# A LoRA-augmented linear layer on one core: rounding and copying in larger pieces, with TensorE looping over groups of 16 rows

## The chip, the core and the metric

The kernel runs on one core of a Trainium2 chip. The core has five engines with queues of their own (TensorE or PE, VectorE or DVE, ScalarE or ACT, GpSimd or POOL, SyncE or SP), and 16 DMA engines move data between the main memory and its on-chip memory. The metric is the device time of one execution in microseconds; lower is better. Before the change the median of three runs is 164.73 us (164.71 to 164.86).

## The reference

`x` is 16 x 2048 x 256 in float32, flattened to 32768 rows of 256. `W` is 256 x 256, `lora_A` 256 x 16, `lora_B` 16 x 256, `lora_E` has 16 numbers and `scale` is 1.

```
y = x_flat @ W
lora_out = ((x_flat @ lora_A) * lora_E) @ lora_B
y = y + scale * lora_out
```

All of it is one product with the 256 x 256 matrix `W + scale * (A * E) @ B`. About 33.5 MB are read and as many written.

## The kernel before

**Rows and chunks.** The 32768 rows are seen as 256 blocks of 128, here called rows for short: one row of the plan is one row of `x` on each of the 128 partitions, 128 KB in all. `PLAN` (line 10) cuts the 256 into seven chunks. A chunk of b rows is one load and one store, in which each partition's part is b KB in one piece. The chunks lie in a ring `xy` of 192 rows in on-chip memory (line 54); the results `y` overwrite the rows of `x` they come from. The first five chunks fill the ring. Chunks 5 and 6 reuse the places of chunks 0, 1 and 2.

**SP's queue** (lines 125 to 136) sets the order of the transfers: `W`, the loads of chunks 0 to 4, the stores 0, 1 and 2, the load of chunk 5 (once stores 0 and 1 have landed), the load of chunk 6 (once store 2 has landed), then the stores 3 to 6. A store is issued when `s_rdy` says that the chunk's last result is in the ring. `lora_A`, `lora_B` and `lora_E` come through ACT's queue (lines 189 to 191).

**The weights.** PE transposes `A` (line 219), DVE multiplies by `E` and `scale` (line 155), PE multiplies by `B` (line 223), DVE adds `W` and rounds to bf16 as `weff` (line 161).

**Steps.** The rows are worked on in steps of Q = 4 rows. DVE rounds eight rows at a time to bf16 into one of two buffers `xb` (line 173), one pair of steps ahead. PE transposes a step's four rows (line 202); bf16 pairs are moved as one float32. DVE copies the transposes from PSUM to `xt` (line 184). PE multiplies: eight matmuls a step, two of them for each row (line 210). ACT copies the step's `y` from PSUM into the ring (line 194), and after a chunk's last step it drains and signals `s_rdy` (line 196). PE's order is written out by hand (`turn`, line 226): the transposes of step k + 1 stand before the products of step k, in a loop over four steps at a time. `ps_xt` and `ps_y` have two halves each; `s_y` counts the copied ones.

**The pause.** Before it rounds the first rows of chunk `PAUSE` = 4, DVE waits until store 2 has landed (line 170). Since it rounds one pair of steps ahead, the last two steps of chunk 3 wait with it. At the start DVE runs 60 empty instructions (line 149).

Of the kernel before, what the change touches and what calls it, by code (L numbers as in the profile page):

```python
# [6 lines left out]

PLAN = [16, 32, 48, 48, 48, 48, 16]  # L10

RING = 192

LEAD = 5
AFTER = {2: [5, 6]}

PAUSE = 4

Q = 4


@with_exitstack
def kernel(
# [11 lines left out]
    P = 128  # L35
    FP32 = mybir.dt.float32
    BF16 = mybir.dt.bfloat16
# [3 lines left out]
    N, K = x_flat.shape  # L41
    M = out_flat.shape[1]
    R = lora_B.shape[0]
    KC = K // P
    CHUNKS = len(PLAN)
    assert K == M == KC * P and sum(PLAN) * P == N and all(b % (2 * Q) == 0 for b in PLAN)

    def sbuf(name, shape, dt):
        return ctx.enter_context(nc.sbuf_tensor(name, shape, dt))

    def psum(name, shape, dt):
        return ctx.enter_context(nc.psum_tensor(name, shape, dt))

    xy = sbuf("xy", [P, RING, K], FP32)

    late = sbuf("late", [P, Q * K], FP32)
    w_sb = late[:, :KC * M].rearrange("p (c m) -> p c m", c=KC)
    b_sb = late[:R, 2 * M:3 * M]
    b_bf = late[:R, 3 * M:3 * M + M // 2].bitcast(BF16)
    ate = late[:R, 3 * M + M // 2:4 * M].bitcast(BF16).rearrange("r (c p) -> r c p", c=KC)  # L60
    xb = [
        sbuf("xb0", [P, 2 * Q, K], BF16)[:],
        late.bitcast(BF16).rearrange("p (j k) -> p j k", k=K),
    ]

    xt = [sbuf(f"xt{s}", [P, Q, P, KC], BF16) for s in range(2)]
    a_sb = sbuf("a_sb", [P, KC, R], FP32)
    e_sb = sbuf("e_sb", [R, 1], FP32)
    weff = sbuf("weff", [P, KC, M], BF16)
    ident = sbuf("ident", [P, P], FP32)  # L70

    ps_xt = [psum(f"ps_xt{s}", [P, Q, P], FP32) for s in range(2)]
    ps_y = [psum(f"ps_y{s}", [P, Q, M], FP32) for s in range(2)]
    ps_at = psum("ps_at", [P, KC, P], FP32)
    ps_aeb = psum("ps_aeb", [P, KC, M], FP32)

    sem = tc.alloc_semaphore
    s_w, s_a, s_b, s_e = sem("s_w"), sem("s_a"), sem("s_b"), sem("s_e")
    s_in = [sem(f"s_in{i}") for i in range(CHUNKS)]
    starts = [sum(PLAN[:i]) for i in range(CHUNKS)]  # L80
    places = [r % RING for r in starts]
    assert sum(PLAN[:LEAD]) <= RING and all(r + b <= RING for r, b in zip(places, PLAN))

    owners = {
        i: [j for j in range(LEAD) if places[j] < places[i] + PLAN[i] and places[i] < places[j] + PLAN[j]]
        for i in range(LEAD, CHUNKS)
# [5 lines left out]
    s_lora = sem("s_lora")  # L92
    s_lpe = sem("s_lpe")
    s_xb = sem("s_xb")
    s_t = sem("s_t")
    s_xt = sem("s_xt")
    s_p = sem("s_p")
    s_y = sem("s_y")
    s_rdy = sem("s_rdy")

    def rows_of(flat, i):
        b, r0 = PLAN[i], starts[i] * P
        return flat[r0:r0 + b * P, :].rearrange("(p b) k -> p b k", b=b)
# [2 lines left out]
        return xy[:, places[i]:places[i] + PLAN[i], :]  # L106


    steps = [(i, r) for i, b in enumerate(PLAN) for r in range(0, b, Q)]

    def rows_of_step(k):
        i, r = steps[k]
        return xy[:, places[i] + r:places[i] + r + Q, :]

    n = len(steps)
    assert n % 4 == 0

    with tc.tile_critical(sync_engine=mybir.EngineType.SP, no_gpsimd_drain=True):  # L118
        sp, pe, dve, act, pool = nc.sync, nc.tensor, nc.vector, nc.scalar, nc.gpsimd


        def load(i):
            sp.dma_start(out=ring_of(i), in_=rows_of(x_flat, i)).then_inc(s_in[i], 16)

        sp.dma_start(out=w_sb, in_=W.rearrange("(p c) m -> p c m", c=KC)).then_inc(s_w, 16)
        for i in range(LEAD):
            load(i)
        for i in range(CHUNKS):
            sp.wait_ge(s_rdy, i + 1)
            sp.dma_start(out=rows_of(out_flat, i), in_=ring_of(i)).then_inc(s_out[min(i, again)], 16)  # L130
            for later in AFTER.get(i, []):
                for j in owners[later]:
                    sp.wait_ge(s_out[j], 16)
                load(later)
        for i in range(len(s_out) - 1):
            sp.wait_ge(s_out[i], 16)


        pool.memset(ident[:], 0.0).then_inc(s_id, 1)  # L139
        pool.wait_ge(s_id, 1)  # L140
        pool.affine_select(  # L141
            out=ident[:], in_=ident[:], compare_op=mybir.AluOpType.not_equal, fill=1.0,
            base=0, pattern=[[-1, P]], channel_multiplier=1,
        ).then_inc(s_id, 1)

        for _ in range(60):
            dve.nop()  # L150
        dve.wait_ge(s_b, 16)
        dve.tensor_copy(out=b_bf, in_=b_sb).then_inc(s_lora, 1)  # L152
        dve.wait_ge(s_e, 16)
        dve.wait_ge(s_lpe, 1)
        dve.tensor_scalar(  # L155
            out=ate, in0=ps_at[:R, :KC, :], scalar1=e_sb[:], scalar2=float(scale),
            op0=mybir.AluOpType.mult, op1=mybir.AluOpType.mult,
        ).then_inc(s_lora, 1)
        dve.wait_ge(s_w, 16)
        dve.wait_ge(s_lpe, 2)  # L160
        dve.tensor_add(out=weff[:], in0=w_sb, in1=ps_aeb[:]).then_inc(s_lora, 1)  # L161

        def round_steps(k):
            i, r = steps[k]
            if r == 0:
                dve.wait_ge(s_in[i], 16)
            if r == 0 and i == PAUSE:
                dve.wait_ge(s_out[again - 1], 16)  # L170
            if k == 2:
                dve.wait_ge(s_lora, 3)
            rounded = dve.tensor_copy(  # L173
                out=xb[k // 2 % 2], in_=xy[:, places[i] + r:places[i] + r + 2 * Q, :],
            )
            if k == 0:
                rounded.then_inc(s_xb, 1)

        round_steps(0)
        for k in range(n):  # L180
            if k % 2 == 0 and k + 2 < n:
                round_steps(k + 2)
            dve.wait_ge(s_t, k + 1)
            dve.tensor_copy(  # L184
                out=xt[k % 2][:].rearrange("w j p c -> w j (p c)"), in_=ps_xt[k % 2][:].bitcast(BF16),
            ).then_inc(s_xt, 1)


        act.dma_start(out=a_sb[:], in_=lora_A.rearrange("(p c) r -> p c r", c=KC)).then_inc(s_a, 16)
        act.dma_start(out=b_sb, in_=lora_B).then_inc(s_b, 16)  # L190
        act.dma_start(out=e_sb[:], in_=lora_E[:, None]).then_inc(s_e, 16)
        for k, (i, r) in enumerate(steps):
            act.wait_ge(s_p, k + 1)
            act.copy(out=rows_of_step(k), in_=ps_y[k % 2][:]).then_inc(s_y, 1)  # L194
            if r + Q == PLAN[i]:
                act.drain().then_inc(s_rdy, 1)

        def transposes(k):  # L200
            for j in range(Q):
                t = pe.transpose(  # L202
                    ps_xt[k % 2][:, j, :], xb[k // 2 % 2][:, k % 2 * Q + j, :].bitcast(FP32), ident[:],
                )
            t.then_inc(s_t, 1)

        def products(k):
            for j in range(Q):
                for c in range(KC):
                    m = pe.matmul(  # L210
                        ps_y[k % 2][:, j, :], xt[k % 2][:, j, :, c], weff[:, c, :],
                        start=(c == 0), stop=(c == KC - 1),
                    )
            m.then_inc(s_p, 1)

        pe.wait_ge(s_a, 16)
        pe.wait_ge(s_id, 2)
        for c in range(KC):
            t = pe.transpose(ps_at[:R, c, :], a_sb[:, c, :], ident[:])  # L219
        t.then_inc(s_lpe, 1)  # L220
        pe.wait_ge(s_lora, 2)
        for c in range(KC):
            m = pe.matmul(ps_aeb[:, c, :], ate[:, c, :], b_bf, start=True, stop=True)  # L223
        m.then_inc(s_lpe, 1)

        def turn(k):
            pe.wait_ge(s_xt, 1).then_inc(s_xt, -1)  # L227
            transposes(k + 1)
            pe.wait_ge(s_y, 1).then_inc(s_y, -1)
            products(k)  # L230

        pe.sem_inc(s_y, 2)
        pe.wait_ge(s_xb, 1)
        transposes(0)
        pe.wait_ge(s_lora, 3)

        with pe.Fori(0, n // 4):
            for k in range(4):
                turn(k)


    with tc.tile_critical(sync_engine=mybir.EngineType.SP, no_gpsimd_drain=True):
        nc.sync.wait_ge(s_out[again], 16 * (CHUNKS - again))

# [1 line left out]
_INS = ['x', 'W', 'lora_A', 'lora_B', 'lora_E', 'scale']  # L246
# [31 lines left out]
```

## Time and profile before

| What | us |
|---|---|
| median of the runs | 164.73 |
| the profiled execution | 166.16 |
| its span, which the profile's times refer to | 164.4 |
| PE busy | 104.0 |
| DVE busy | 79.6 |
| ACT busy | 66.2 |
| ACT's copy of `y`, 128x1024 f32, mean of 64 | 1.014 |
| DVE's copy of transposes, 128x1024 bf16, mean of 64 | 0.688 |
| DVE's rounding, 128x2048 to bf16, mean of 32 | 1.218 |
| DVE's wait for store 2 at the pause | 19.7 |

The profile is one execution, and its own time differs from the median of the runs. Its slices cut the span into 40 equal parts; a digit is the share of a slice in which an engine was busy, in tenths. PEclk is the clock granted to TensorE in tenths of full speed. An entry in the list of waits names who waited, for whom, how long in all, how often, and the longest. A DMA issue is listed with the time from its issue to its landing, which includes the time it stands behind others. In a table of windows each line gives start and end, then the busy time and number of instructions of PE, PEld, DVE, ACT and POOL, the granted clock, the DMA engines' share and GB/s.

### The profile page before, as it was taken

How to read it: one execution, taken by the hardware profiler on the slowest of the kernel's cores; microseconds unless marked ns; L12 is line 12 of the kernel's file. 1: busy time of each engine (PE TensorE's matmuls, PEld its weight loads, DVE VectorE, ACT ScalarE, POOL GpSimd, SP SyncE). 2: the span in 40 equal slices, each digit the busy share in tenths (PEclk: the TensorE clock that was granted, in tenths of full speed). 3: DMA queues.
4: the chain of work that ended last, by engine and by line, in shares of the span. 5: the costliest groups of instructions: out<-in, count | busy, mean ns of one | idle time of the engine just before them, and what ended most of it. 6: DMA issues, size and time to landing. Idle time of an engine off the chain costs nothing. (4 is left out here: it accounts for less than half of the span.)

```text
span 164.4 us, 1979 instructions
## 1 busy us (share of the span) xinstructions
PE 104.0 (63%) x776; PEld 80.6 (49%) x776; DVE 79.6 (48%) x99; ACT 66.2 (40%) x65; POOL 0.7 (0%) x6
## 2 busy tenths in 40 slices
PE   1039199899989998991000099999899899900000
PEld 0017178677767777770000087777777677700000
DVE  0181355768867886750000456788678767300000
ACT  3002224565666666563000026666656565620000
POOL 1000000000000000000000000000000000000000
PEclk9999957999999999999555559999999999975555
DMA  4999989998999898999899999899989999998970
GB/s 156 431 459 431 510 383 395 490 455 383 395 550 395 383 383 371 451 455 447 383 514 443 383 397 490 351 462 498 395 383 433 502 407 395 443 490 383 395 327 16
DMA packets 2370, 67.42 MB, mean 410 GB/s; under 512 B 432, under 2 KB 448, under 8 KB 576
## 3 DMA queue, kind: packets, MB, share of 16 engines
q1 hardware_dynamic: 2160, 67.37, 95.8%
q10 hardware_dynamic: 208, 0.03, 0.2%
q14 instruction: 2, 0.02, 0.0%
HBM read 33.85 MB, written 33.55 MB: 410 GB/s over the span
## 5 line engine op out<-in xcount | busy, mean ns | idle before, releaser
L194 ACT COPY xy<-ps_y 128x1024 f32<-128x1024 f32 x64 | 64.9, 1014 | 76.6 <-PE ps_y L210 76.6
L210 PE MATMUL ps_y<-weff,xt 128*128 128x256 bf16 x512 | 70.3, 283 | 0.0
L184 DVE COPY xt<-ps_xt 128x1024 bf16<-128x1024 bf16 x64 | 44.0, 688 | 30.6 <-PE ps_xt L202 30.5
L210 PEld LDWEIGHTS ps_y<-weff,xt 128*128 128x128 bf16 x512 | 52.1, 102 | 6.8
L202 PE MATMUL ps_xt<-ident,late 128*128 128x128 f32 x128 | 21.4, 293 | 26.7 <-PEq L227 26.7
L202 PEld LDWEIGHTS ps_xt<-ident,late 128*128 128x128 f32 x128 | 14.4, 148 | 34.5 <-issue 34.5
L173 DVE CAST xb<-xy 128x2048 bf16<-128x2048 f32 x16 | 19.5, 1218 | 24.3 <-DMA out_dram<-xy 19.7
L202 PE MATMUL ps_xt<-ident,xb 128*128 128x128 f32 x132 | 22.8, 300 | 5.9 <-PEq L227 3.9
L202 PEld LDWEIGHTS ps_xt<-ident,xb 128*128 128x128 f32 x132 | 15.8, 153 | 13.9 <-issue 11.1
L173 DVE CAST late<-xy 128x2048 bf16<-128x2048 f32 x16 | 19.5, 1217 | 0.0
L223 PE MATMUL ps_aeb<-late 16*128 16x256 bf16 x2 | 0.6, 404 | 3.8 <-DVE late L155 3.8
L219 PE MATMUL ps_at<-ident,a_sb 128*16 128x128 f32 x2 | 0.6, 402 | 3.5 <-DMA a_sb<-in_lora_A_dram 3.5
L152 DVE CAST late<-late 16x256 bf16<-16x256 f32 x1 | 0.3, 280 | 4.4 <-DMA late<-in_lora_B_dram 4.4
L223 PEld LDWEIGHTS ps_aeb<-late 16*128 16x128 bf16 x2 | 0.1, 106 | 4.3 <-DVE late L155 4.3
L194 ACT ACT_TABLE_LOAD x1 | 1.3, 1283 | 2.3 <-issue 2.3
L219 PEld LDWEIGHTS ps_at<-ident,a_sb 128*16 128x16 f32 x2 | 0.1, 90 | 3.5 <-DMA a_sb<-in_lora_A_dram 3.5
L155 DVE TENSOR_SCALAR late<-ps_at,e_sb 16x256 bf16<-16x256 f32 x1 | 0.5, 471 | 2.8 <-DMA e_sb<-in_lora_E_dram 2.8
L161 DVE TENSOR_TENSOR weff<-late,ps_aeb 128x512 bf16<-128x512 f32 x1 | 0.7, 687 | 0.8 <-PE ps_aeb L223 0.8
L141 POOL TENSOR_SCALAR_AFFINE_SELECT ident<-ident 128x128 f32<-128x128 f32 x1 | 0.3, 294 | 0.2 <-POOL ident L139 0.2
L139 POOL MEMSET ident<- 128x128 f32 x1 | 0.2, 205 | 0.5 <-SPq L118 0.5
L259 POOL MEMSET const-bfloat16-1.0<- 128x1 bf16 x1 | 0.1, 102 | 0.0
L259 POOL MEMSET const-uint8-127<- 128x1 uint8 x1 | 0.1, 102 | 0.0
(2 smaller groups left out, 0.2 us busy)
## 6 DMA issues: line engine op xcount, KB each, us to landing
xy<-in_x_dram SPq DMA_DIRECT2D x4, 6144.0 KB, 38.2
out_dram<-xy SPq DMA_DIRECT2D x4, 6144.0 KB, 26.1
xy<-in_x_dram SPq DMA_DIRECT2D x2, 2048.0 KB, 14.4
xy<-in_x_dram SPq DMA_DIRECT2D x1, 4096.0 KB, 17.1
out_dram<-xy SPq DMA_DIRECT2D x2, 2048.0 KB, 29.3
out_dram<-xy SPq DMA_DIRECT2D x1, 4096.0 KB, 37.8
late<-in_W_dram SPq DMA_DIRECT2D x1, 256.0 KB, 2.9
a_sb<-in_lora_A_dram ACTq DMA_DIRECT2D x1, 16.0 KB, 2.6
```

The source lines that it names most:

```text
L139: pool.memset(ident[:], 0.0).then_inc(s_id, 1)
L141: pool.affine_select(out=ident[:], in_=ident[:], compare_op=mybir.AluOpType.not_equal, fill=1.0, base=0, pattern=[[-1, P]], channel_multip ...
L152: dve.tensor_copy(out=b_bf, in_=b_sb).then_inc(s_lora, 1)
L155: dve.tensor_scalar(out=ate, in0=ps_at[:R, :KC, :], scalar1=e_sb[:], scalar2=float(scale), op0=mybir.AluOpType.mult, op1=mybir.AluOpType.mult,
L161: dve.tensor_add(out=weff[:], in0=w_sb, in1=ps_aeb[:]).then_inc(s_lora, 1)
L173: rounded = dve.tensor_copy(out=xb[k // 2 % 2], in_=xy[:, places[i] + r:places[i] + r + 2 * Q, :],)
L184: dve.tensor_copy(out=xt[k % 2][:].rearrange("w j p c -> w j (p c)"), in_=ps_xt[k % 2][:].bitcast(BF16),).then_inc(s_xt, 1)
L194: act.copy(out=rows_of_step(k), in_=ps_y[k % 2][:]).then_inc(s_y, 1)
L202: t = pe.transpose(ps_xt[k % 2][:, j, :], xb[k // 2 % 2][:, k % 2 * Q + j, :].bitcast(FP32), ident[:],)
L210: m = pe.matmul(ps_y[k % 2][:, j, :], xt[k % 2][:, j, :, c], weff[:, c, :], start=(c == 0), stop=(c == KC - 1),)
L219: t = pe.transpose(ps_at[:R, c, :], a_sb[:, c, :], ident[:])
L223: m = pe.matmul(ps_aeb[:, c, :], ate[:, c, :], b_bf, start=True, stop=True)
```

## The change

The plan becomes 16, 32, 48, 48, 32, 48, 32, and the ring 176 rows. DVE rounds G = 16 rows into the one buffer `xb`, and copies the transposes of S = 8 rows at a time. `ps_xt` then holds eight rows in each half; `ps_at` and `ps_aeb` share PSUM with `ps_y`. PE waits for `weff` before its first transpose and then loops over groups of 16 rows: all transposes of the group, then its products in four pieces of Q = 4 rows. ACT copies the first 58 pieces of `y`, and DVE the last `LATE` = 6, after all its other work. The last copy of a chunk signals `s_rdy` itself, without a drain; GpSimd passes that signal on to `s_y`, which is now one semaphore for each half of `ps_y`. The small inputs move to SP's queue: `lora_A` before chunk 0, `lora_B` and `lora_E` behind it. GpSimd rounds `lora_B`. The 60 empty instructions go.

```diff
-PLAN = [16, 32, 48, 48, 48, 48, 16]
-RING = 192
+PLAN = [16, 32, 48, 48, 32, 48, 32]
+RING = 176
...
-Q = 4
+G, S, Q = 16, 8, 4
+LATE = 6
...
-    late = sbuf("late", [P, Q * K], FP32)
...
-    xb = [
-        sbuf("xb0", [P, 2 * Q, K], BF16)[:],
-        late.bitcast(BF16).rearrange("p (j k) -> p j k", k=K),
-    ]
-    xt = [sbuf(f"xt{s}", [P, Q, P, KC], BF16) for s in range(2)]
+    xb = sbuf("xb", [P, G, K], BF16)
+    xt = [sbuf(f"xt{s}", [P, S, P, KC], BF16) for s in range(2)]
...
-    ps_xt = [psum(f"ps_xt{s}", [P, Q, P], FP32) for s in range(2)]
+    ps_xt = [psum(f"ps_xt{s}", [P, S, P], FP32) for s in range(2)]
     ps_y = [psum(f"ps_y{s}", [P, Q, M], FP32) for s in range(2)]
...
+    ps_at = ps_y[0][:R, 0, :].rearrange("r (c p) -> r c p", c=KC)
+    ps_aeb = ps_y[1][:, :KC, :]
...
-    s_y = sem("s_y")
+    s_y = [sem(f"s_y{h}") for h in range(2)]
...
+        sp.dma_start(out=a_sb[:], in_=lora_A.rearrange("(p c) r -> p c r", c=KC)).then_inc(s_a, 16)
+        load(0)
+        sp.dma_start(out=b_sb[:], in_=lora_B).then_inc(s_b, 16)
+        sp.dma_start(out=e_sb[:], in_=lora_E[:, None]).then_inc(s_e, 16)
+        for i in range(1, LEAD):
             load(i)
...
+        pool.wait_ge(s_b, 16)
+        pool.tensor_copy(out=b_bf[:], in_=b_sb[:]).then_inc(s_lora, 1)
...
+        copies = pieces(Q)
+        def y_of(q, engine, copy):
+            i, r = copies[q]
+            engine.wait_ge(s_p, q + 1)
+            done = copy(out=rows_at(i, r, Q), in_=ps_y[q % 2][:])
+            if r + Q == PLAN[i]:
+                done.then_inc(s_rdy, 1)
+            else:
+                done.then_inc(s_y[q % 2], 1)
+        for i in range(CHUNKS - 1):
+            pool.wait_ge(s_rdy, i + 1).then_inc(s_y[((starts[i] + PLAN[i]) // Q - 1) % 2], 1)
+        for q in range(len(copies) - LATE):
+            y_of(q, act, act.copy)
...
+        for g, (i, r) in enumerate(pieces(G)):
             if r == 0:
                 dve.wait_ge(s_in[i], 16)
             if r == 0 and i == PAUSE:
                 dve.wait_ge(s_out[again - 1], 16)
...
+            dve.tensor_copy(out=xb[:], in_=rows_at(i, r, G)).then_inc(s_xb, 1)
+            for k in range(g * G // S, (g + 1) * G // S):
+                dve.wait_ge(s_t, k + 1)
+                dve.tensor_copy(
+                    out=xt[k % 2][:].rearrange("w j p c -> w j (p c)"), in_=ps_xt[k % 2][:].bitcast(BF16),
+                ).then_inc(s_xt, 1)
+        for q in range(len(copies) - LATE, len(copies)):
+            y_of(q, dve, dve.tensor_copy)
...
-        act.dma_start(out=a_sb[:], in_=lora_A.rearrange("(p c) r -> p c r", c=KC)).then_inc(s_a, 16)
-        act.dma_start(out=b_sb, in_=lora_B).then_inc(s_b, 16)
-        act.dma_start(out=e_sb[:], in_=lora_E[:, None]).then_inc(s_e, 16)
...
-                act.drain().then_inc(s_rdy, 1)
...
         def products(k):
+            for h in range(S // Q):
+                pe.wait_ge(s_y[h], 1).then_inc(s_y[h], -1)
+                for j in range(Q):
+                    for c in range(KC):
+                        m = pe.matmul(
+                            ps_y[h][:, j, :], xt[k % 2][:, h * Q + j, :, c], weff[:, c, :],
+                            start=(c == 0), stop=(c == KC - 1),
+                        )
+                m.then_inc(s_p, 1)
...
-        def turn(k):
-            pe.wait_ge(s_xt, 1).then_inc(s_xt, -1)
-            transposes(k + 1)
-            pe.wait_ge(s_y, 1).then_inc(s_y, -1)
-            products(k)
...
         pe.wait_ge(s_lora, 3)
-        with pe.Fori(0, n // 4):
-            for k in range(4):
-                turn(k)
+        with pe.Fori(0, sum(PLAN) // G):
+            pe.wait_ge(s_xb, 1).then_inc(s_xb, -1)
+            for k in range(G // S):
+                transposes(k)
+            for k in range(G // S):
+                pe.wait_ge(s_xt, 1).then_inc(s_xt, -1)
+                products(k)
```

More of the change, by code (lines that the diff above doesn't have):

```diff
@@ L45 @@
     CHUNKS = len(PLAN)
-    assert K == M == KC * P and sum(PLAN) * P == N and all(b % (2 * Q) == 0 for b in PLAN)
+    assert K == M == KC * P and sum(PLAN) * P == N and all(b % G == 0 for b in PLAN)
     def sbuf(name, shape, dt):
@@ L54 @@
     xy = sbuf("xy", [P, RING, K], FP32)
-    late = sbuf("late", [P, Q * K], FP32)
[L57 to L60, printed above, removed]
-    xb = [
-        sbuf("xb0", [P, 2 * Q, K], BF16)[:],
-        late.bitcast(BF16).rearrange("p (j k) -> p j k", k=K),
-    ]
-    xt = [sbuf(f"xt{s}", [P, Q, P, KC], BF16) for s in range(2)]
+    xb = sbuf("xb", [P, G, K], BF16)
+    xt = [sbuf(f"xt{s}", [P, S, P, KC], BF16) for s in range(2)]
+    w_sb = sbuf("w_sb", [P, KC, M], FP32)
     a_sb = sbuf("a_sb", [P, KC, R], FP32)
+    b_sb = sbuf("b_sb", [R, M], FP32)
     e_sb = sbuf("e_sb", [R, 1], FP32)
+    b_bf = sbuf("b_bf", [R, M], BF16)
+    ate = sbuf("ate", [R, KC, P], BF16)
     weff = sbuf("weff", [P, KC, M], BF16)
     ident = sbuf("ident", [P, P], FP32)
-    ps_xt = [psum(f"ps_xt{s}", [P, Q, P], FP32) for s in range(2)]
+    ps_xt = [psum(f"ps_xt{s}", [P, S, P], FP32) for s in range(2)]
     ps_y = [psum(f"ps_y{s}", [P, Q, M], FP32) for s in range(2)]
-    ps_at = psum("ps_at", [P, KC, P], FP32)
-    ps_aeb = psum("ps_aeb", [P, KC, M], FP32)
+    ps_at = ps_y[0][:R, 0, :].rearrange("r (c p) -> r c p", c=KC)
+    ps_aeb = ps_y[1][:, :KC, :]
     sem = tc.alloc_semaphore
@@ L106, in ring_of, with pieces, rows_at @@
         return xy[:, places[i]:places[i] + PLAN[i], :]
[L109 to L116, printed above, removed]
+    def pieces(rows):
+        return [(i, r) for i, b in enumerate(PLAN) for r in range(0, b, rows)]
+    def rows_at(i, r, rows):
+        return xy[:, places[i] + r:places[i] + r + rows, :]
     with tc.tile_critical(sync_engine=mybir.EngineType.SP, no_gpsimd_drain=True):
@@ L123, in load @@
             sp.dma_start(out=ring_of(i), in_=rows_of(x_flat, i)).then_inc(s_in[i], 16)
-        sp.dma_start(out=w_sb, in_=W.rearrange("(p c) m -> p c m", c=KC)).then_inc(s_w, 16)
-        for i in range(LEAD):
+        sp.dma_start(out=w_sb[:], in_=W.rearrange("(p c) m -> p c m", c=KC)).then_inc(s_w, 16)
+        sp.dma_start(out=a_sb[:], in_=lora_A.rearrange("(p c) r -> p c r", c=KC)).then_inc(s_a, 16)
[3 more added lines that the diff above has]
+        for i in range(1, LEAD):
             load(i)
@@ L144 @@
         ).then_inc(s_id, 1)
[L149 to L152, printed above, removed]
+        pool.wait_ge(s_b, 16)
[13 more added lines that the diff above has]
+            y_of(q, act, act.copy)
         dve.wait_ge(s_e, 16)
@@ L155 @@
         dve.tensor_scalar(
-            out=ate, in0=ps_at[:R, :KC, :], scalar1=e_sb[:], scalar2=float(scale),
+            out=ate[:], in0=ps_at, scalar1=e_sb[:], scalar2=float(scale),
             op0=mybir.AluOpType.mult, op1=mybir.AluOpType.mult,
@@ L160 @@
         dve.wait_ge(s_lpe, 2)
-        dve.tensor_add(out=weff[:], in0=w_sb, in1=ps_aeb[:]).then_inc(s_lora, 1)
-        def round_steps(k):
-            i, r = steps[k]
+        dve.tensor_add(out=weff[:], in0=w_sb[:], in1=ps_aeb).then_inc(s_lora, 1)
+        for g, (i, r) in enumerate(pieces(G)):
             if r == 0:
@@ L170, in round_steps @@
                 dve.wait_ge(s_out[again - 1], 16)
[L171 to L186, printed above, removed]
@@ L189 @@
-        act.dma_start(out=a_sb[:], in_=lora_A.rearrange("(p c) r -> p c r", c=KC)).then_inc(s_a, 16)
-        act.dma_start(out=b_sb, in_=lora_B).then_inc(s_b, 16)
-        act.dma_start(out=e_sb[:], in_=lora_E[:, None]).then_inc(s_e, 16)
[L192 to L196, printed above, removed]
+            dve.tensor_copy(out=xb[:], in_=rows_at(i, r, G)).then_inc(s_xb, 1)
@@ L200, in transposes @@
+            for k in range(g * G // S, (g + 1) * G // S):
[5 more added lines that the diff above has]
+            y_of(q, dve, dve.tensor_copy)
         def transposes(k):
[L201 to L204, printed above, removed]
+            for j in range(S):
+                t = pe.transpose(ps_xt[k % 2][:, j, :], xb[:, k * S + j, :].bitcast(FP32), ident[:])
@@ L205, in transposes @@
             t.then_inc(s_t, 1)
         def products(k):
[L208 to L214, printed above, removed]
+            for h in range(S // Q):
[7 more added lines that the diff above has]
+                m.then_inc(s_p, 1)
@@ L216 @@
+        for h in range(2):
+            pe.sem_inc(s_y[h], 1)
         pe.wait_ge(s_a, 16)
@@ L218 @@
         for c in range(KC):
-            t = pe.transpose(ps_at[:R, c, :], a_sb[:, c, :], ident[:])
+            t = pe.transpose(ps_at[:, c, :], a_sb[:, c, :], ident[:])
         t.then_inc(s_lpe, 1)
@@ L222 @@
         for c in range(KC):
-            m = pe.matmul(ps_aeb[:, c, :], ate[:, c, :], b_bf, start=True, stop=True)
+            m = pe.matmul(ps_aeb[:, c, :], ate[:, c, :], b_bf[:], start=True, stop=True)
         m.then_inc(s_lpe, 1)
-        def turn(k):
-            pe.wait_ge(s_xt, 1).then_inc(s_xt, -1)
-            transposes(k + 1)
-            pe.wait_ge(s_y, 1).then_inc(s_y, -1)
-            products(k)
-        pe.sem_inc(s_y, 2)
-        pe.wait_ge(s_xb, 1)
-        transposes(0)
-        pe.wait_ge(s_lora, 3)
-        with pe.Fori(0, n // 4):
-            for k in range(4):
-                turn(k)
+        pe.wait_ge(s_lora, 3)
+        with pe.Fori(0, sum(PLAN) // G):
[5 more added lines that the diff above has]
+                products(k)
     with tc.tile_critical(sync_engine=mybir.EngineType.SP, no_gpsimd_drain=True):
```

## The prediction

> **What bounds the kernel now.** I read the slices first, because they show which resource is never idle, then the queue table, the waits of the queue that issues the transfers, the chain, and last narrow windows over the start and the end.
>
> ```profile
> DMA  4999989998999898999899999899989999998970
> DMA packets 2370, 67.42 MB, mean 410 GB/s; under 512 B 432, under 2 KB 448, under 8 KB 576
> ...
> q1 hardware_dynamic: 2160, 67.37, 95.8%
> ...
> PE ps_y L210 2%; PE ps_xt L202 2%; ACT xy L194 1%
> ```
>
> The DMA row is full from the second slice to the last but one; SP's queue holds the 16 DMA engines 95.8% of the span. The chain of work covers only 5% of the span: it ends with ScalarE's last copy at 145.03 us, and what follows is no engine's work but stores.
>
> ```profile
> SPq L130 <- ACTq L196: 105.9, 7, 23.4
> SPq L133 <- DMA out_dram<-xy: 18.0, 1, 18.0
> SPq L273 <- DMA out_dram<-xy: 16.8, 1, 16.8
> SPq L123 <- DMA out_dram<-xy: 14.2, 1, 14.2
> ```
>
> SP's sequencer does wait for copies (first line), but the transfers don't: a store that is issued lands 18 to 41 us later, since it stands behind others. The third line is the end: 16.8 us of waiting for stores already issued.
>
> ```profile
> 144.00:152.00 8.00, 0.00 (x0) 0.00 (x0) 0.00 (x0) 1.01 (x1) 0.00 (x0) 0.64 0.97 418
> ...
> 159.00:160.00 1.00, 0.00 (x0) 0.00 (x0) 0.00 (x0) 0.00 (x0) 0.00 (x0) 0.50 0.35 148
> 160.00:161.00 1.00, 0.00 (x0) 0.00 (x0) 0.00 (x0) 0.00 (x0) 0.00 (x0) 0.50 0.15 66
> 161.00:162.00 1.00, 0.00 (x0) 0.00 (x0) 0.00 (x0) 0.00 (x0) 0.00 (x0) 0.50 0.08 33
> ```
>
> Windows over the end (the last two columns are DMA share and GB/s): compute is over, and from 159 us only one or two of the 16 DMA engines still move bytes. So the bound is one queue, first in first out on each DMA engine, and inside it the engine that lags most.
>
> The packet records behind these windows give the budget. A 16, 32 or 48 KB packet takes 0.611, 1.213 or 1.815 us, and each engine carries eight of each load and store. Before: 16 x (2 x 0.611 + 1.213 + 4 x 1.815) = 155.1 us an engine. First x packets start at 3.2 to 3.8 us; 3.5 + 155.1 = 158.6. Most engines end at 159.3 to 159.8, the last at 162.6; it lands at 163.1 and the span ends at 164.4. What the last engine lost over 158.6 is 4.0 us: about 0.75 where the first stores follow the loads (its 48 KB packets at 60 us take 2.2 to 3.0), 1.2 on one packet at 93.6, 0.75 where loads turn to stores at 110 us, and 1.3 from store packets that take 1.90 for 1.82 as long as compute runs beside them, on one engine only.
>
> **The change, part by part.** PLAN 16 32 48 48 48 48 16 becomes 16 32 48 48 32 48 32. An engine's packets cost 16 x (0.611 + 3 x 1.213 + 3 x 1.815) = 155.1 us: **the same to a tenth**, with the same 14 big transfers and three turns between loads and stores. What can move is the edge.
>
> *Start.* lora_A's DMA goes ahead of chunk 0 on SP. Its issue took 0.39 us on ACT's queue; chunk 0 is issued at 1.38, its first packets follow W's (last W packet at 3.41). So the cost lies between 0 (W still fills the engines) and 0.45 us; I take 0.2. lora_B and E follow chunk 0: per engine a packet of 0.05 and one of 0.01 us, which ran before too, on the other queue, where the first chunk 0 packets beside them took up to 1.23 for 0.61. Between -0.2 and +0.2; I take 0. Their landing moves from 7.41 us (E) to about 10, behind chunk 0; the weights, by the rows between 7.43 and 9.36, are done 2 us later, at about 12, and TensorE now waits for them before its first transpose. That delays compute alone, which has the pause as cover (below).
>
> *DVE.* The rounding: 256 columns take 280 ns, 2048 take 1217, so 0.523 ns a column and 4096 take 2.29 us (for two of 1.22). The transposes' copy: 0.69 for 1024 columns, 1.22 for 2048 by the same slope (bounds 0.69 and 1.38). 4.73 us per 16 rows against 5.19. All of it lies beside transfers.
>
> *The new order on PE.* Four transposes take 0.63 and eight matmuls 0.87 at full clock (last chain), so 16 rows need 2.52 + 3.48 = 6.0, as before. But there is one xb, and products wait inside the group: copy of half one ends at 1.26 + 0.04 + 1.22 = 2.5, products start at 2.65 (0.12 from copy to the next PE work, as at 142.34 to 142.46). ps_y's two banks now go back by s_y[0] and s_y[1]: ScalarE's 1.01 per copy holds products 3 and 4 to about 4.7 and 5.7, the group ends at 6.6, and the next rounding (3.8 to 6.1) is ready. Period 6.65 for 6.02: nine groups lose 6 us, off the path. GpSimd's relay of s_y at a chunk's end (cost not in the trace; its nearest rows are 0.1 to 0.3 us) has some 3.5 us until that bank is wanted. Behind the PE waits stands all of PE, and ScalarE for it.
>
> *Pause.* Chunks 0 to 3: first transposes at 12.1 + 2.3 = 14.4, a cold group of at most 12 us (1.09 and 1.91 per four and eight), eight of 6.65: done by 80. Store 2 lands 16 rows of loads earlier: 92.6 - 4.8 = 88. So DVE still waits there, some 8 us for 19.7. Nothing of chunk 3 is left behind the pause any more (before, its last eight rows were); its store then only stands in the queue.
>
> *End.* From 88: rounding 2.3, 2 lost to the slow clock (94.6 to 98.5 ran at 1.91 per eight products), six groups of 6.65, then the last. There DVE copies the last six pieces, after its own work. A 128x1024 f32 copy from PSUM on DVE isn't in the trace; by rows it lies between 0.69 (the bf16 copy) and 1.37 (twice the 512-column f32 add with a PSUM operand). The add is the nearer row, f32 from PSUM as this copy is; twice it less one start of 0.15 (the rounding's line at no columns) makes 1.2. The group then lasts 3.8 + 6 x 1.2 = 11. Sum 143; the last store is issued at about 143 instead of 145.1. It has 32 rows now, 9.7 us of packets, so the queue runs dry before it at some 150 on the fast engines and 152.5 on the last. With 1.05 us from issue to first packet (W: 0.94 to 1.99) the slack is **6 to 8 us, for 13 before**. The drains that go (1.04 each) ended with the copies, and give nothing.
>
> The Trainium skill ("VectorE: DVE Perf Modes", the errata section on SBUF-source ops) gives 120 plus one cycle a column at 0.96 GHz for an f32 PSUM source, as an estimate 1.19 us for this piece; with it the sum would end in the same place.
>
> *Turns.* The loads that meet stores first are now 32 KB packets, not 48 (0.75 lost at 48, a tenth on average at 16): between -0.65 and 0, I take -0.3. Those at the second turn are 32 KB, not 16: between 0 and +0.65, I take +0.3. *The lagging engine* loses 0.05 per us of stores beside compute: first half 58 to 80 for 63 to 75, second 113 to 143 for 112 to 145: +10 us less 3, +0.35 at most, 0 if compute is not the cause; I take 0.15.
>
> Sum: 0.2 + 0 - 0.3 + 0.3 + 0.15 = **+0.35 us**. Against the profiled execution (166.16, its span 164.4 and 1.8 around it) that is 166.5; against the median of 164.73, which lies 1.4 below that execution, 165.1.
>
> The clock: PE runs at granted 1.00 with 7.3 to 7.5 of 8 us busy; I get 6.0 of 6.65, gaps of 0.1 to 0.3 us. The Trainium skill speaks against this order ("TensorE: Matmul & The Clock Gate", "A second HAM failure mode"): small idle gaps between groups that cycle PSUM banks made the clock swing. By the row there is no loss, by the rule the second rival's.
>
> **Rivals.**
> 1. *The lag at the restart doesn't recur* (the other side: faster). Six packets near 93.6 us, just as DVE restarts and chunk 6's load is issued, lose up to 1.23 us, on the very engine that ends last. The other ten lost nothing. If the restart at 88 falls between packets, the last engine ends 0.8 to 1.2 earlier: 165.1 - 1.1 = 164.0. It decides once that engine loses under 0.5 there. For it: no such loss at other issues (78, 100, 119 us). Against: restart and issue come together again. 22%.
> 2. *Compute becomes late.* If a group takes over 7.8 us, the pause vanishes and the last store finds an empty queue. A clock swinging between the halves makes a group (6.65 + 12)/2 = 9.3: 92.3 + 6 x 9.3 + 13 = 161, plus 1 + 9.7 + 3 = 175 span end, some 10 us slower; 167 if only the last groups suffer. Against: the steady 1.00. 8%.
> 3. *The turns cost more*: 48 KB stores meeting 32 KB loads lose on all engines what was lost at 60 us, with the other terms at their upper ends: 165.1 + 0.3 + 0.35 + 0.2 + 0.25 = 166.2 (first turn, second turn, lagging engine, start). 20%.
>
> **How the numbers follow.** The forecast, 164.7 to 165.5, has 50%. Low end: rival 1 with start and lagging engine at no cost, 163.7; high end: rival 3 and one more turn's loss of 0.75, 166.9; rival 2 is left out. About 0.2% (0.33 us) is what a measurement can tell from no change, so 164.40 to 165.06 is the same: 0.21 of the forecast's 0.50. Faster 0.22 (rival 1), slower 0.29 + 0.20 + 0.08 = 0.57.
>
> **What would show it.** Right: DMA slices full as before, queue share near 95%, a wait of DVE for a store of about 8 us, the last store issued near 143, the same tail after 159. Wrong: a DMA hole before the last store, PEclk under 9 outside start and pause, a group period over 7.8 us, or the last DMA engines ending together with the others.

## The result, and the profile after

The changed kernel takes 165.98 us (median of 7, 165.25 to 166.79) where the kernel before takes 164.72 (164.55 to 164.90): a ratio of **1.007, interval 1.0043 to 1.0097**, slower by about 1.2 us. Its executions also differ by 1.5 us among each other, where those of before differ by 0.35. The profiled one is its shortest, 165.25 with a span of 163.5, while that of before, 166.16, lies above all seven timed ones; so the two spans can't be set against each other, only their parts.

The page of the changed kernel, slices and queue:

```profile
DMA  5999999899999989999999998999998999999991
...
q1 hardware_dynamic: 2368, 67.40, 96.7%
...
DVE 1%; PE 1%; issue 0%
```

Still one full queue, and a chain of 2% that ends at 144.7 us. The new order of work is not where the time went. The waits of SP's queue and then those of the engines (who, for whom, us in total, times, longest):

```profile
SPq L129 <- DVE xy L154: 16.9, 1, 16.9
SPq L132 <- DMA out_dram<-xy: 16.2, 1, 16.2
SPq L265 <- DMA out_dram<-xy: 16.2, 1, 16.2
```

```profile
DVE xb L184 <- DMA out_dram<-xy: 15.8, 1, 15.8
DVE ate L170 <- DMA e_sb<-in_lora_E_dram: 10.4, 1, 10.4
```

SP waits for DVE's last copy and then 16.2 us for stores already issued (16.8 before); DVE still has 15.8 us of pause. So compute stays ahead of the queue, although `lora_E` now lands at 10.4 us.

What did change stands at the very start. The first line is the changed kernel's window from 2 to 9 us, the second that of before; the last two columns are the DMA engines' share and GB/s:

```profile
2.00:9.00 7.00, 0.59 (x2) 0.10 (x2) 0.00 (x0) 0.18 (x1) 0.00 (x0) 1.00 1.06 396
```

```profile
2.00:9.00 7.00, 1.20 (x4) 0.23 (x4) 1.08 (x3) 1.28 (x1) 0.00 (x0) 1.00 1.04 415
```

(396 - 415) x 7 us is 0.13 MB that is not moved in these 7 us. On average that is 0.3 us of queue. But a DMA engine that falls behind at the start has its eight packets of every transfer to move all the same, and carries the delay on. The records of landings show it: chunk 0's sixteen parts land between 8.72 and 10.00 us in the changed kernel and between 8.48 and 9.24 before, chunk 3's between 47.81 and 48.85 against 47.26 and 48.01. The lag is kept as far as chunk 3. What was issued when shows in SP's own lines (start, duration), first of the changed kernel, then of before, where chunk 0 is the first of the five loads:

```profile
1.38 0.43 SPq L121 DMA_DIRECT2D a_sb<-in_lora_A_dram  x1
1.86 0.42 SPq L118 DMA_DIRECT2D xy<-in_x_dram  x1
```

```profile
1.38 2.65 SPq L123 DMA_DIRECT2D xy<-in_x_dram  x5
```

### The profile page after: what moved, and what is told of

Same layout as the page of the kernel before. It is cut to its first block, busy times and chain, and to the rows that moved or that the text cites. A ratio compares the mean times of both kernels' runs of the same rounds, so it can differ in the third digit from the quotient of the medians.

```text
span 163.5 us, 1907 instructions
## 1 busy us (share of the span) xinstructions
PE 97.1 (59%) x772; PEld 79.6 (49%) x772; DVE 81.7 (50%) x56; ACT 57.2 (35%) x59; POOL 1.1 (1%) x7
## 5 line engine op out<-in xcount | busy, mean ns | idle before, releaser
L154 ACT COPY xy<-ps_y 128x1024 f32<-128x1024 f32 x58 | 56.0, 1016 | 73.7 <-PE ps_y L205 73.7
L205 PE MATMUL ps_y<-weff,xt 128*128 128x256 bf16 x512 | 64.2, 279 | 16.9 <-PEq L202 16.9
L205 PEld LDWEIGHTS ps_y<-weff,xt 128*128 128x128 bf16 x512 | 48.0, 100 | 32.5 <-issue 24.5
L188 DVE COPY xt<-ps_xt 128x2048 bf16<-128x2048 bf16 x32 | 37.9, 1220 | 32.3 <-PE ps_xt L197 32.3
L184 DVE CAST xb<-xy 128x4096 bf16<-128x4096 f32 x16 | 36.6, 2286 | 18.2 <-DMA out_dram<-xy 15.8
L197 PE MATMUL ps_xt<-ident,xb 128*128 128x128 f32 x256 | 34.1, 292 | 19.1 <-PEq L225 19.1
L197 PEld LDWEIGHTS ps_xt<-ident,xb 128*128 128x128 f32 x256 | 31.4, 151 | 20.3 <-issue 20.1
L154 DVE COPY xy<-ps_y 128x1024 f32<-128x1024 f32 x6 | 7.2, 1220 | 1.4 <-PE ps_y L205 1.3
L170 DVE TENSOR_SCALAR ate<-ps_y,e_sb 16x256 bf16<-16x256 f32 x1 | 0.5, 471 | 10.4 <-DMA e_sb<-in_lora_E_dram 10.4
L220 PE MATMUL ps_y<-b_bf,ate 16*128 16x256 bf16 x2 | 0.6, 402 | 6.5 <-DVE ate L170 6.5
L176 DVE TENSOR_TENSOR weff<-w_sb,ps_y 128x512 bf16<-128x512 f32 x1 | 0.7, 686 | 0.8 <-PE ps_y L220 0.8
```

The lines of the kernel that those rows point to most:

```text
L154: done = copy(out=rows_at(i, r, Q), in_=ps_y[q % 2][:])
L170: dve.tensor_scalar(out=ate[:], in0=ps_at, scalar1=e_sb[:], scalar2=float(scale), op0=mybir.AluOpType.mult, op1=mybir.AluOpType.mult,).the ...
L176: dve.tensor_add(out=weff[:], in0=w_sb[:], in1=ps_aeb).then_inc(s_lora, 1)
L184: dve.tensor_copy(out=xb[:], in_=rows_at(i, r, G)).then_inc(s_xb, 1)
L188: dve.tensor_copy(out=xt[k % 2][:].rearrange("w j p c -> w j (p c)"), in_=ps_xt[k % 2][:].bitcast(BF16),).then_inc(s_xt, 1)
L197: t = pe.transpose(ps_xt[k % 2][:, j, :], xb[:, k * S + j, :].bitcast(FP32), ident[:])
```

## The experiments

Theory: the three small transfers in SP's queue hold up the first chunk, the last DMA engine carries that to the end, and the new order of work and the new plan cost nothing. Rivals: the 32 KB packets where loads and stores meet; or only the choice of executions that were compared.

**The same two kernels again.** No edit.

> The kernel before, unchanged, once more: how far two sets of executions of one kernel differ. Theory 'the difference is real': ratio 1.000 within 0.002, and a profiled span that is 0.5 to 1.5 us above what its median allows, as the 164.4 shown. Rival 'the difference lies in which executions were compared': a median of 165.5 or more, like the 166.16 of the first profiled execution.

164.92 us, ratio 1.0015 (0.9996 to 1.0034); profiled span 163.0. So 164.4 was an unusual span. In this execution no packet near 93.6 us loses over 0.4 us, where the first lost 1.2 on one engine: that loss differs from execution to execution of one kernel. These two sets of executions of one kernel differ by 0.34% at most.

> The changed kernel, unchanged, once more. If the difference is real: 165.5 to 166.5 and again a spread of over 1 us between its executions. If not: 164.7 within 0.4.

165.51 us, ratio 1.0049 (1.0029 to 1.0069), executions from 165.18 to 166.79. The difference is real, and so is its spread. The profiled execution is its longest (span 165.0), and it moved less at the start than the first:

```profile
2.00:9.00 7.00, 0.60 (x2) 0.10 (x2) 0.00 (x0) 0.19 (x1) 0.00 (x0) 1.00 0.97 356
```

Here chunk 0's parts land between 8.76 and 10.24 us.

**The plan alone.**

```diff
-PLAN = [16, 32, 48, 48, 48, 48, 16]
-RING = 192
+PLAN = [16, 32, 48, 48, 32, 48, 32]
+RING = 176
```

> The kernel before with only the new plan and ring of 176 rows. Theory 'start' (three small transfers in SP's queue cost 0.8 us): 164.7, no difference. Rival 'turns' (32 KB packets where loads and stores meet): about 165.5 to 166.

164.60 us, ratio 0.9992 (0.9980 to 1.0004). The new turns by themselves are no cause. By the landing records the last engine spends 0.45 us over its packets' time on chunk 4 (10.15 for 9.70) where the second execution of the kernel before spends 0.63 (15.15 for 14.52), and 0.20 on chunks 5 and 6 together, where the old plan takes 0.68.

**The small transfers back on ACT's queue,** in the changed kernel.

```diff
-        sp.dma_start(out=a_sb[:], in_=lora_A.rearrange("(p c) r -> p c r", c=KC)).then_inc(s_a, 16)
-        load(0)
-        sp.dma_start(out=b_sb[:], in_=lora_B).then_inc(s_b, 16)
-        sp.dma_start(out=e_sb[:], in_=lora_E[:, None]).then_inc(s_e, 16)
-        for i in range(1, LEAD):
+        for i in range(LEAD):
             load(i)
...
+        act.dma_start(out=a_sb[:], in_=lora_A.rearrange("(p c) r -> p c r", c=KC)).then_inc(s_a, 16)
+        act.dma_start(out=b_sb[:], in_=lora_B).then_inc(s_b, 16)
+        act.dma_start(out=e_sb[:], in_=lora_E[:, None]).then_inc(s_e, 16)
```

> The changed kernel with lora_A, lora_B and lora_E issued from ACT's queue as before. Theory 'start': 165.2, and chunk 1 lands at 19.0 us instead of 19.8. Rival 'turns': 166.0, no gain.

164.59 us, ratio 0.9987 (0.9974 to 1.0001): the whole difference is gone, with the new order of work and the new plan in place. Chunk 1 lands at 19.0 us. From chunk 3's last landing to chunk 4's it is 10.25 us here; in both profiled executions of the changed kernel it is 11.0, against 9.70 of packets. So part of the loss falls where the loads of chunk 4 first meet stores. The same stretch takes 10.6 to 11.0 us in each of the four profiled executions of this plan with a small transfer ahead of chunk 0, and 9.8 to 10.3 in the five without.

**The move alone,** in the kernel before: the same three transfers into SP's queue, in the changed kernel's order.

> The kernel before with only the three small transfers moved into SP's queue as in the change. If this move carries the whole difference: 165.6 within 0.3, and a spread over its executions of more than 1 us. Rival, it costs only together with the new order of work: 164.8.

166.57 us, ratio 1.0082 (1.0053 to 1.0111), above the expected range and no less than the changed kernel itself (1.007 and 1.0049). On this chip the kernel before takes 165.25, which is part of the excess. The move carries the difference. The executions spread by 1.0 us (165.92 to 166.94), at the edge of what was expected. The same window of this kernel, 50 GB/s under the kernel before:

```profile
2.00:9.00 7.00, 0.60 (x2) 0.10 (x2) 0.00 (x0) 0.18 (x1) 0.00 (x0) 1.00 1.00 365
```

**Which of the three.** First `lora_A` alone back on ACT's queue, then `lora_B` and `lora_E` alone.

```diff
-        sp.dma_start(out=a_sb[:], in_=lora_A.rearrange("(p c) r -> p c r", c=KC)).then_inc(s_a, 16)
...
+        act.dma_start(out=a_sb[:], in_=lora_A.rearrange("(p c) r -> p c r", c=KC)).then_inc(s_a, 16)
```

> The changed kernel with lora_A alone back on ACT's queue. Theory 'A ahead' (its 128 packets of 128 B stand before chunk 0 on the same queue): 164.6, chunk 0 landed by 9.3 us. Theory 'B and E' (small packets between chunk 0 and chunk 1): 165.5. Theory 'issue' (SP's issues of the later loads come later and hold up chunk 0's packets while they run): 165.1, chunk 0 landed at 9.7.

164.80 us beside 165.25 of the kernel before on that chip, ratio 0.9970 (0.9949 to 0.9991). Chunk 0 landed at 9.2 us.

```diff
-        sp.dma_start(out=b_sb[:], in_=lora_B).then_inc(s_b, 16)
-        sp.dma_start(out=e_sb[:], in_=lora_E[:, None]).then_inc(s_e, 16)
...
+        act.dma_start(out=b_sb[:], in_=lora_B).then_inc(s_b, 16)
+        act.dma_start(out=e_sb[:], in_=lora_E[:, None]).then_inc(s_e, 16)
```

> The changed kernel with lora_B and lora_E alone back on ACT's queue. Theory 'A ahead': 165.5, chunk 0 landed at 10.0 us or later. Theory 'B and E': 164.6. Theory 'issue': 164.9, chunk 0 landed at 9.5.

165.91 us, ratio 1.0043 (1.0013 to 1.0072), 362 GB/s from 2 to 9 us, and chunk 0 landed at 11.3 us. So it is the transfer that goes ahead of chunk 0, and not the two behind it.

**Later issues of the other loads,** in the kernel before.

```diff
-        for i in range(LEAD):
+        load(0)
+        sp.wait_ge(s_w, 16)
+        for i in range(1, LEAD):
             load(i)
```

> The kernel before; SP waits for W to land (about 3.8 us) before it issues the loads of chunks 1 to 4. Theory 'issue': 165.3 or more, with slow packets of chunk 0 between 4 and 8 us. Theories 'A ahead' and 'B and E': 164.8, no difference, since chunk 0 covers the later issues until 9 us.

165.37 us, but the kernel before took 165.25 on that chip: ratio 1.0016 (0.9998 to 1.0034). No packet of chunk 0 after 4 us loses more than 0.04 us, and 416 GB/s are moved from 2 to 9 us. The theory that SP's issues hold up packets finds no support.

**Small packets, or the place.** First `lora_A` behind chunk 0, then `lora_B` (16 packets of 1 KB) in its place ahead of chunk 0, with `lora_A` on ACT's queue.

```diff
-        sp.dma_start(out=a_sb[:], in_=lora_A.rearrange("(p c) r -> p c r", c=KC)).then_inc(s_a, 16)
         load(0)
+        sp.dma_start(out=a_sb[:], in_=lora_A.rearrange("(p c) r -> p c r", c=KC)).then_inc(s_a, 16)
         sp.dma_start(out=b_sb[:], in_=lora_B).then_inc(s_b, 16)
```

> The changed kernel with lora_A behind chunk 0 in SP's queue (order W, chunk 0, A, B, E). Theory 'small packets anywhere in SP's queue': 165.5 or more. Theory 'delay' (anything that holds chunk 0's issue back by 0.45 us) and theory 'small packets ahead': 164.7.

164.70 us, ratio 0.9986 (0.9969 to 1.0002). The 128 small packets cost nothing behind chunk 0.

```diff
-        sp.dma_start(out=a_sb[:], in_=lora_A.rearrange("(p c) r -> p c r", c=KC)).then_inc(s_a, 16)
+        sp.dma_start(out=b_sb[:], in_=lora_B).then_inc(s_b, 16)
         load(0)
-        sp.dma_start(out=b_sb[:], in_=lora_B).then_inc(s_b, 16)
...
+        act.dma_start(out=a_sb[:], in_=lora_A.rearrange("(p c) r -> p c r", c=KC)).then_inc(s_a, 16)
```

> The changed kernel with lora_A on ACT's queue and lora_B in lora_A's place ahead of chunk 0: the same later issue of chunk 0, but 16 packets of 1 KB for 128 of 128 B. Theory 'delay': 165.5, chunk 0 landed at 10 us. Both theories of small packets: 164.7, chunk 0 landed by 9.5.

165.71 us, ratio 1.0055 (1.0035 to 1.0075). So **the place decides, not the packets**. This execution shows the loss best. Half-microsecond windows, first of this kernel, then of the changed kernel with all three on ACT's queue:

```profile
3.50:4.00 0.50, 0.50 (x2) 0.08 (x2) 0.00 (x0) 0.00 (x0) 0.00 (x0) 1.00 0.57 164
4.00:4.50 0.50, 0.07 (x1) 0.00 (x0) 0.00 (x0) 0.00 (x0) 0.39 (x1) 1.00 0.60 229
4.50:5.00 0.50, 0.00 (x0) 0.00 (x0) 0.00 (x0) 0.00 (x0) 0.00 (x0) 1.00 0.78 328
```

```profile
3.50:4.00 0.50, 0.49 (x2) 0.10 (x2) 0.00 (x0) 0.08 (x1) 0.00 (x0) 1.00 1.03 367
4.00:4.50 0.50, 0.10 (x1) 0.00 (x0) 0.00 (x0) 0.00 (x0) 0.01 (x1) 1.00 0.84 360
4.50:5.00 0.50, 0.00 (x0) 0.00 (x0) 0.00 (x0) 0.00 (x0) 0.38 (x1) 1.00 1.08 459
```

The share before the last column is what to see: in the first kernel a third of the DMA engines is idle from 3.5 to 5 us, with chunk 0 issued at 1.86. The packet records agree: five of the 16 engines start their first packet of chunk 0 at 5.0 to 5.2 us, ten between 2.97 and 3.54, one at 4.04. `lora_B`'s 16 packets have all been moved by 3.54, so it is not they that keep the five engines until 5 us. With chunk 0 issued right behind W, at 1.38 us, none starts after 4.2. At the end of the same execution (one line for each microsecond, this kernel, then the one with all three on ACT's queue) more engines are still at work; the 164 GB/s from 160 to 161 us are five packets of 32 KB, as many as engines started late:

```profile
159.00:160.00 1.00, 0.00 (x0) 0.00 (x0) 0.00 (x0) 0.00 (x0) 0.00 (x0) 0.50 0.61 262
160.00:161.00 1.00, 0.00 (x0) 0.00 (x0) 0.00 (x0) 0.00 (x0) 0.00 (x0) 0.50 0.38 164
161.00:162.00 1.00, 0.00 (x0) 0.00 (x0) 0.00 (x0) 0.00 (x0) 0.00 (x0) 0.50 0.08 33
```

```profile
159.00:160.00 1.00, 0.00 (x0) 0.00 (x0) 0.00 (x0) 0.00 (x0) 0.00 (x0) 0.50 0.08 33
160.00:161.00 1.00, 0.00 (x0) 0.00 (x0) 0.00 (x0) 0.00 (x0) 0.00 (x0) 0.50 0.00 0
161.00:162.00 1.00, 0.00 (x0) 0.00 (x0) 0.00 (x0) 0.00 (x0) 0.00 (x0) 0.50 0.00 0
```

**lora_B and lora_E behind chunk 0,** in the kernel before.

```diff
-        for i in range(LEAD):
+        load(0)
+        sp.dma_start(out=b_sb, in_=lora_B).then_inc(s_b, 16)
+        sp.dma_start(out=e_sb[:], in_=lora_E[:, None]).then_inc(s_e, 16)
+        for i in range(1, LEAD):
             load(i)
...
-        act.dma_start(out=b_sb, in_=lora_B).then_inc(s_b, 16)
-        act.dma_start(out=e_sb[:], in_=lora_E[:, None]).then_inc(s_e, 16)
```

> The kernel before with lora_B and lora_E in SP's queue behind chunk 0, lora_A left on ACT's. If what made the changed kernel with lora_A on ACT's queue 0.3% faster than before is that these two no longer run beside chunk 0's first packets: 0.997 of the kernel before. If it was the new order of work or the plan: 1.000.

164.86 us, ratio 0.9992 (0.9976 to 1.0007): no gain that can be told from none.

**Half of the products,** in the changed kernel with `lora_A` on ACT's queue.

```diff
-                    for c in range(KC):
-                        m = pe.matmul(
-                            ps_y[h][:, j, :], xt[k % 2][:, h * Q + j, :, c], weff[:, c, :],
-                            start=(c == 0), stop=(c == KC - 1),
-                        )
+                    m = pe.matmul(
+                        ps_y[h][:, j, :], xt[k % 2][:, h * Q + j, :, 0], weff[:, 0, :],
+                        start=True, stop=True,
+                    )
```

> The changed kernel with lora_A on ACT's queue, and only the first of the two products of each row (the second half of the sum over the 256 inputs is left out): half of TensorE's matmuls and weight loads for the products, all else the same. Theory 'the slowest DMA engine is slowed by TensorE's work': its loss per 48 KB store packet falls from 0.09 to about 0.05 us, and the time to 164.3. Rival, by ScalarE's or VectorE's work: 0.09 and 164.7.

163.93 us, ratio 0.9936 (0.9914 to 0.9958), for 0.9970 (0.9949 to 0.9991) with all the products; the intervals just overlap. The loss of the slowest engine on store 3's 48 KB packets falls only from 0.081 to 0.067 us on average (six packets each); all its losses on stores from 113 us on fall from 1.0 to 0.7. TensorE's work may have a part in it, less than expected. Six packets of one execution each don't show it, and the work of the other engines was not tried.

## Why the prediction was right and where it was not

**The number.** The sum gave +0.35 us; the two sets measured +1.2 and +0.8 (ratios 1.007 and 1.0049). 165.98 lies above the forecast of 164.7 to 165.5. That it lies within the outer bounds, 163.7 to 166.9, is luck: the upper bound was added up from turns made dearer by the new packets, and the excess comes from the start.

**The bound.** Right: one queue, first in first out on each engine, and the engine that lags most sets the end. The kernels that moved 350 to 396 GB/s from 2 to 9 us are those that measured 1.004 to 1.008; the others moved 411 to 416 and measured 1.002 or less. One reading was off: the share of 0.35 from 159 to 160 us is five or six engines still at work, not one or two, and two from 160.

**Packets and plan.** Right for the plan alone, which measured 0.9992. The two turns were costed at -0.3 and +0.3; the landings of one execution each give -0.2 and -0.5 on the last engine, the medians -0.13 us for the plan as a whole (-0.33 to +0.07). In the changed kernel the last engine loses 1.3 us at the first turn, not 0.45. All four executions of the new plan with a small transfer ahead lose more there, and why was not tested.

**Start.** The step that was mis-sized. I bounded `lora_A`'s place ahead of chunk 0 by the time of its issue, 0.45 us at most, and took 0.2. The move of the three alone costs 0.0082 of 164.7, 1.35 us (0.9 to 1.8), in the kernel before, and 0.9 us in the changed kernel (165.51 with it, 164.59 without). The direction and the transfer were right. The bound took one delay for all 16 engines, with nothing to follow from it, and the runs show otherwise. In the execution with `lora_B` ahead, five engines start chunk 0 at least 1.5 us after ten others. In the changed kernel's own two executions the latest first packets begin at 4.07 and 4.39 us, little later than before (4.04 and 4.14). Eight packets at 0.611 us from there would end at 8.96 and 9.28; the last ones end at 9.57 and 9.89, so there the packets themselves take longer, which they don't on the last engine before (8.93 reckoned, 8.91 ended). At the first turn the last engine then loses 0.8 us more than with the three on ACT's queue. How late chunk 0 is differs from execution to execution: its last part landed at 10.0 and 10.2 us in the changed kernel, at 10.6, 11.2 and 11.3 in the three other kernels with a small transfer ahead of it. A likely reason for the spread of the changed kernel's times, argued and not shown, since the records don't name the engines: an execution is long where the delay hits the engine that later loses 1 us on its stores. `lora_B` and `lora_E` were costed at 0, and behind chunk 0 they cost nothing that was measured.

The Trainium skill ("DMA: Bandwidth & Descriptors", section "Issuing engines are not separate DMA queues") says that issuing from several engines saves only the time of the issue, usually small against the transfer. Here that time is 0.43 us for `lora_A`, and the way back to ACT's queue for the three gained 0.9 us in the changed kernel; the measurement decides.

**DVE and PE.** Right, and off the path. The changed kernel's rows (count, then busy us and mean ns):

```profile
L188 DVE COPY xt<-ps_xt 128x2048 bf16<-128x2048 bf16 x32 | 37.9, 1220 | 32.3 <-PE ps_xt L197 32.3
L184 DVE CAST xb<-xy 128x4096 bf16<-128x4096 f32 x16 | 36.6, 2286 | 18.2 <-DMA out_dram<-xy 15.8
...
L154 DVE COPY xy<-ps_y 128x1024 f32<-128x1024 f32 x6 | 7.2, 1220 | 1.4 <-PE ps_y L205 1.3
```

1.22, 2.29 and 1.2 us were predicted. The figure of the Trainium skill for the third ("VectorE: DVE Perf Modes", the errata section on SBUF-source ops), an estimate of 1.19 us, is 2% below the measured 1.22. The period of a group, from the timeline (start, duration, engine):

```profile
99.83 1.91 PE L197 MATMUL ps_xt<-ident,xb 128*128 128x128 f32 x16
100.90 2.35 DVE L188 COPY xt<-ps_xt 128x2048 bf16<-128x2048 bf16 x2 [2.31 <-PE ps_xt L197]
102.42 1.91 PE L205 MATMUL ps_y<-weff,xt 128*128 128x256 bf16 x16 [0.69 <-PEq L202]
...
106.43 1.91 PE L197 MATMUL ps_xt<-ident,xb 128*128 128x128 f32 x16
```

From 99.83 to 106.43 it is 6.60 us (6.65 predicted). The last store was issued at 144.8 instead of 143. The last group began 0.7 us later than reckoned (132.9 for 132.2) and took 11.9 us instead of 11; in it the clock was at half between 137.7 and 141.2 us, and DVE waited 1.3 us for products. The slack covered it.

**Pause.** 15.8 us against 8. I let the whole first group run at the slow clock, 12 us as an upper bound, and it took 7.6. I also counted to the end of the ninth group (76.6 us), while DVE's own part of it ends at 73.3. And store 2 landed at 88.95 us instead of 88.

**The lagging engine.** Costed at +0.15, and it went the other way: its losses on stores after 112 us add up to 1.2 and 1.1 us in the two profiled executions of the changed kernel, 1.4 and 1.6 in those of before. Nor is it always the last: followed by their times, its packets run to the last end in the second execution of before, but only to 161.94 us with `lora_B` ahead, where another engine ends at 162.41.

**Rivals.** The condition of the first came true: in neither execution of the changed kernel does a packet between 80 and 100 us lose more than 0.15 us. No gain came of it. The loss near 93.6 us differs among executions of the old order too (1.23, 0.37, and 0.96 with the later loads), and the median it was taken off already lay 1.4 us below the execution that had it. The second did not happen: the clock was 1.00 from 18 to 76 us with TensorE busy 48.5 of 58. The rows are the window, and the last group's first products with TensorE's idle time before them:

```profile
18.00:76.00 58.00, 48.49 (x414) 40.13 (x413) 37.86 (x25) 33.05 (x35) 0.00 (x0) 1.00 1.01 427
```

```profile
137.58 4.45 PE L205 MATMUL ps_y<-weff,xt 128*128 128x256 bf16 x24 [2.80 <-PEq L202]
```

The Trainium skill's rule of a clock that swings with small gaps ("TensorE: Matmul & The Clock Gate", "A second HAM failure mode") doesn't show here: gaps of 0.3 to 0.7 us in every group left the clock at 1.00, and while compute ran on it fell only once, at 137.7 us, after a gap of 2.8 us in which TensorE waited for DVE's copies (the first of them ends at 137.4). The third had the place of the loss partly right (the start at its upper end, and the first turn), and the wrong mechanism: with the new plan alone the turn costs 0.45 us.

**A version that may beat both.** The changed kernel with `lora_A` on ACT's queue measured 0.9970 (0.9949 to 0.9991) of the kernel before. That is little, and its near twins (all three on ACT's queue, or `lora_A` behind chunk 0) measured 0.9987 and 0.9986, which can't be told from none. Which of its parts would give it is open, as the plan alone and the two transfers behind chunk 0 alone gave 0.9992 each.

**Open.** Why engines start late when a transfer stands between W and the first large load: the later issue and the transfer itself were not separated (a later issue with no transfer ahead was not run). Why chunk 0's packets take longer then, and why the first turn costs more. And what else beside TensorE slows one DMA engine on stores.

## What to carry to other kernels

In a kernel that is one full DMA queue, the first large load goes out as early as it can; small inputs go behind it, or through another queue. A short delay there is not paid once on average but by the engine that it hits worst, and a queue that is full to the end leaves no idle time to make it up. Here compute that ended well before the queue could be reordered without loss, and any gain was 0.3% at most as measured.

## What the runs showed of the hardware

One DMA engine of the 16 takes 1.90 us for a 48 KB store packet, the others 1.82, as long as compute runs. The engine that ends last ends 0.3 to 1.5 us after the second last in the 14 profiled executions. With a packet of 1 KB on each engine ahead of the first large load, five of the 16 engines stood idle until 5 us, though all these packets had been moved by 3.54. Two profiled executions of one kernel differ by 1.4 us (before) and 1.5 us (changed) in span with no change in the code.
